# A diffusion layer's front: the order of context's sums of squares, of the query norms and of the chunk transpositions

## The chip, the cores and the metric

One NeuronCore of one Trainium2 chip. The time is the device time of one execution in microseconds (us), as the median of several runs. The engines are named as in the profile: PE (TensorE), DVE (VectorE), ACT (ScalarE), POOL (GpSimd), and SP, which issues most of the DMAs. PEld is the loading of weights into TensorE.

## The reference

One layer of a diffusion backbone on 512 latent tokens and 256 context tokens, D = 1024. What the change touches:

```python
h  = rms_norm(x, g_norm1) * (1.0 + sc1) + sh1          # latents
hc = rms_norm(ctx, g_norm1) * (1.0 + csc1) + csh1      # context; sc, sh from silu(c) @ w_ada
aq, ak, av, dq, dk, dv, dz, da, db, ga, gd = split_cols(h @ w_in)      # the same for hc
q_a = axial_rope(rms_norm(heads(aq, 8), q_norm_g), row, col)   # windowed attention
k_a = axial_rope(rms_norm(heads(ak, 2), k_norm_g), row, col)
o_dl = bidir_delta(...)     # gated DeltaNet, chunks of 64; each needs a triangular inverse
x_new = x + gt1 * merge(y_attn, o_dl, dz, ga, gd)
x_new = x_new + gt2 * mlp(x_new, sh2, sc2)
```

## The kernel before

Everything is held transposed, with features on the 128 partitions and tokens along the free axis. A product in full precision is made of three products of rounded halves: high by high, high by low and low by high (`split`, `wload`, `modulate`).

**How instructions get their order.** The program is traced in Python, and a planner then puts each engine's instructions in a fixed order at build time. Of the instructions that are ready in its own model of time, it takes the one that stands first in the program. So an instruction can stand ahead of others that come before it in the program, if the planner takes it to be ready earlier. What was planned runs in that order on its engine: one that is not ready on the chip holds up all behind it. `tc.add_manual_dep(..., nosync)` adds an edge that binds the planner only. `pm` uses it to chain TensorE's matmuls of the front in the very order of the program; a plain `PE.matmul` is not in that chain.

**The front** (lines 239 to 420). The modulation vectors come from `w_ada`, loaded in eight pieces of 1 MB (`wada(kt)`). For each of the eight feature tiles `kt`: `strip(kt)` multiplies the condition by its piece (16 TensorE instructions), `columns(kt)` turns the row into columns `modA` and `modS` by way of one ACT copy (L263), `latent(kt)` normalises and modulates the latents (L350 on DVE, L351 on ACT, L352 on DVE, L373 on ACT), and `big(kt, tiles...)` multiplies them into up to four accumulators of the DeltaNet's keys, three matmuls a tile. They are software pipelined: step `kt` of the loop issues columns(kt+1), strip(kt+2), latent(kt+1), big(kt, 0, 1, 2, 3). The matmuls of `strip`, `columns` and `big` go through `pm`.

`rms` makes the reciprocal root of a mean square: squares on ACT (L308), additions on DVE (L311), a matmul with ones that sums over the partitions (L313), then Ln and Exp on ACT (through `act`, L148). Context's is called in step 3 behind big(3, ...), with plain `PE.matmul`. `context(i)` modulates one of eight feature tiles of the context (L350, L351, L352, L364), two of them behind each of the steps 4 to 7. `ab_strips` multiplies latents, and behind big(7) context, by the small gate weights.

**Attention's inputs beside the chunk matrices** (lines 862 to 1041). `weave` runs two generators side by side in proportion to their numbers of steps. `mats` normalises the DeltaNet's keys and calls `chunk_mats(gi)` for three groups of chunks. Each makes products of keys in two banks `kk` (L850), decays by matmuls (L875, L876), and DVE products of both (L870, L874, L886, L888, L895, and last L896, which writes `NTO[gi]` and is the last reader of `kk`). `attn_in` goes through six tiles: the keys, three query tiles, the values, the last query tile. `in_tile_steps` yields behind every two of the eight feature tiles: a tile of latents alone has four matmuls to such a step in its first half, one with context eight. The previous tile's `finish` (k_attn, q_attn, v_attn) is called behind the first step of the next tile; q_attn and k_attn begin with `qk_norm`: square (ACT, L491), scaled copy (L492), a matmul that sums over a head (L494), rotation on DVE (L497 to L500), Ln, Exp, product (L505). The weights of a tile are cut by ACT (L280 high part, L286 the negated copy that a DMA then adds to).

Behind the weave, `fw` (L906) and `bw` (L909) transpose the first group's matrix on DVE, their sum (L1041) goes to `invert`, and two more pairs of transpositions follow before the second inversion.

Of the kernel before, what the change touches and what calls it, by code (L numbers as in the profile page):

```python
# [12 lines left out]
ALU = mybir.AluOpType  # L13
# [10 lines left out]
ATT = 32  # L24
NHALF = 3
CTXAT = 3
WARM = 3, 6, 4, 4
NONES = 16
AHEAD = 2
# [10 lines left out]
SEQ = 512  # L40
CTX = 256
# [4 lines left out]
HC = CH // 2  # L46
# [53 lines left out]
def tile_layer(ctx: ExitStack, tc: tile.TileContext, I: dict, out: bass.AP, dbg=None):  # L100
    nc = tc.nc
    V, A, G, PE = nc.vector, nc.scalar, nc.gpsimd, nc.tensor
# [19 lines left out]
    alloc, bank = mem.get, lambda n=1: banks.get(n * 512)  # L122
# [14 lines left out]
    nosync = mybir.DependencyInfo(mybir.DependencyClass.NoSync, mybir.DependencyReason.DATA)  # L137
    actg = {"set": None, "head": None, "ops": []}

    def act(out_, in_, func, **kw):  # L140

        sets = TABLES.get(func)
        if sets and actg["set"] not in sets:
            head = A.preload_act_table_set(sets[0])
            for o in actg["ops"]:
                tc.add_manual_dep(head.ins, o.name, nosync, reason="table sets")
            actg.update(set=sets[0], head=head.ins, ops=[head.ins])
        r = A.activation(out_, in_, func, **kw)  # L148
        if sets:
            tc.add_manual_dep(r.ins, actg["head"].name, nosync, reason="table sets")  # L150
            actg["ops"].append(r.ins)
        return r
# [4 lines left out]
    ones = const.tile([P, P], F32, name="ones")  # L157
# [61 lines left out]
    def strip(kt):  # L219

        if kt < 2:
            rps.append(banks.get(512, True))
        rp_ = rps[kt % 2]
        wb = wbs[kt % 4]
        for half in range(2):
            for g in range(4):
                k = half * 4 + g
                pm(rp_[32 * g:32 * g + 32, :256], scond[:, k], wb[:, k * 256:(k + 1) * 256],
                   start=(half == 0), stop=(half == 1))
        if kt < 4:  # L230
            wada(kt + 4)
        if kt > 3:
            wb.free()

    def warm(kt, n):

        for _ in range(n):
            pm(rps[kt % 2][:, 384:512], ones, ones, start=True, stop=True)

    xs_, cs_ = alloc(8 * SEQ), alloc(8 * CTX)  # L240
# [59 lines left out]
    rstd = alloc(768)  # L300
    rx, rc = rstd[:, :512], rstd[:, 512:768]

    def rms(src, nt, n, r):

        ss = bank()
        for i in range(nt):
            b = alloc(1024)
            A.activation(b.ap, src[:, i * 1024:(i + 1) * 1024], AF.Square)  # L308
            w = 512
            while w >= n:  # L310
                V.tensor_tensor(b[:, :w], b[:, :w], b[:, w:2 * w], op=ALU.add)  # L311
                w //= 2
            PE.matmul(ss[:, :n], ones, b[:, :n], start=(i == 0), stop=(i == nt - 1))  # L313
            b.free()
        act(r, ss[:, :n], AF.Ln, bias=epsc, scale=1.0 / D)
        ss.free()
        act(r, r, AF.Exp, scale=-0.5)

    rms(xs_, 4, SEQ, rx)
    strip(0)  # L320
    warm(0, WARM[0])
    columns(0)
# [26 lines left out]
    def modulate(t, src, r, sc, sh, hi, lo, eng=V):  # L349
        V.scalar_tensor_tensor(t, src, sc, r, op0=ALU.mult, op1=ALU.mult)  # L350
        A.activation(r32(hi), t, AF.Identity, bias=sh)  # L351
        eng.scalar_tensor_tensor(r32(lo), t, sh, hi, op0=ALU.add, op1=ALU.subtract)  # L352
        return r32(hi), r32(lo)
# [4 lines left out]
    def context(kt):  # L358

        t = alloc(256)  # L360
        o = kt * 512
        hc.append(modulate(t.ap, ct_[kt], rc, modA[:, kt, 1:2], modS[:, kt, 1:2],
                           HCb[:, o:o + 256], HCb[:, o + 256:o + 512]))
        tc_.append((t, A.activation(t.ap, t.ap, AF.Identity, bias=modS[:, kt, 1:2])))  # L364
# [11 lines left out]
    def big(kt, *tiles):  # L376

        for i in tiles:
            w, acc = early[i]
            for j, (x, y) in enumerate(((0, 0), (0, 1), (1, 0))):  # L380
                pm(acc.ap, w[x][:, kt, :], hx[kt][y], start=(kt == j == 0), stop=(kt == KT - 1 and j == 2))

    latent(0)
    load_early()
    warm(1, WARM[1])
    columns(1)
# [18 lines left out]
    for kt in range(3, KT):  # L405
        if kt + 1 < KT:
            columns(kt + 1)
        if kt + 2 < KT:
            strip(kt + 2)
        if kt + 1 < KT:  # L410
            latent(kt + 1)
        if kt == 5:
            abx = bank()
            ab_strips(abx.ap, tx, 0)
        big(kt, 0, 1, 2, 3)
        if kt == 3:
            rms(cs_, 2, CTX, rc)
        if kt > 3:
            for i in range(2):
                context(2 * kt - 8 + i)  # L420
    hold.append(tx[-1][1])
    ab_strips(abx.ap, tx, 1)
    abc = bank()
# [320 lines left out]
    t, t2 = alloc(TOK), alloc(TOK)  # L744
# [51 lines left out]
    for n in range(2):  # L796
        m = A.activation(trr[:, 2 * n:2 * n + 2], tri[:, 8 * n:8 * n + 2], AF.Copy)
# [6 lines left out]
    m = V.tensor_copy(maskb, mt.ap.rearrange("p (d k) -> p d k", d=2))  # L804
# [31 lines left out]
    NTO = [alloc(512, True) for _ in range(3)]  # L836
    v3 = lambda ap, n=HC: ap.rearrange("p (m i) -> p m i", i=n)
# [15 lines left out]
    def diag_off(dst):  # L853

        v = dst.ap.rearrange("p (m x i) -> p x m i", x=2, i=HC)
        return v[:, 0], v[:, 1]

    def chunk_mats(gi):
        ms = slice(gi * 16, gi * 16 + 16)
        kk = bank(2)  # L860
        kD, kO = diag_off(kk)
        for _ in half_products(kk, gi, kT):
            for _ in range(HPAUSE):
                yield
        yield
        dO = bank()
        for d in range(2):
            mg, mb = alloc(1024), alloc(512)
            row = lambda m_: m_[:, d, :].unsqueeze(1).broadcast_to([P, 16, HC])
            V.tensor_tensor(v3(mb.ap), row(nmask), bc(btok[:, d, ms], HC), op=ALU.mult)  # L870
            dp = bank()
            for x in range(2):
                gx = mg[:, x * 512:x * 512 + 512]
                V.tensor_tensor(v3(r32(gx)), row(mi), bc(gsp[:, x, d, ms], HC), op=ALU.mult)  # L874
                PE.matmul(dp.ap, trr[:, d, :], r32(gx), start=(x == 0), stop=(x == 1))  # L875
                PE.matmul(dO.ap, trr[:, 2 + d, :], r32(gx), start=(d == x == 0), stop=(d == x == 1))  # L876
            mg.free()
            if gi == 0:
                eb = alloc(512)
                e, na = eb.ap, neg[0][:, d * 512:d * 512 + 512]  # L880
            else:
                o = (gi - 1) * 512
                e, na = ED[d][:, o:o + 512], neg[1 + d][:, o:o + 512]
            act(e, dp.ap, AF.Exp)
            dp.free()
            V.tensor_tensor(e, e, mb.ap, op=ALU.mult)  # L886
            mb.free()
            V.tensor_tensor(v3(na), v3(e), kD, op=ALU.mult)  # L888
            if gi == 0:
                eb.free()  # L890
            yield
        eb = alloc(512) if gi == 0 else None
        e = eb.ap if gi == 0 else EO[:, (gi - 1) * 512:gi * 512]
        act(e, dO.ap, AF.Exp)
        V.tensor_tensor(v3(e), v3(e), bc(tbO[:, ms], HC), op=ALU.mult)  # L895
        V.tensor_tensor(v3(NTO[gi].ap), v3(e), kO, op=ALU.mult)  # L896
        for b in (kk, dO, eb):
            if b:
                b.free()
        yield  # L900


    mat = lambda ap: ap.rearrange("p (r s) -> p r s", s=HC)

    def fw(src, t):
        V.transpose(mat(t), src.rearrange("p (m i) -> p i m", i=HC))  # L906

    def bw(src, t):
        V.transpose(t.rearrange("p (j i) -> p i j", i=HC), src.rearrange("p (m i) -> p i m", i=HC))  # L909

    X, X3 = [], []

# [97 lines left out]
    def attn_in():  # L1010
        qs = [lambda acc, j=j: q_attn(acc, j) for j in range(4)]
        todo = [(T_AK, k_attn)] + [(T_AQ + j, qs[j]) for j in range(3)] + [(T_AV, v_attn), (T_AQ + 3, qs[3])]
        done = None
        for ti, finish in todo:
            g = in_tile_steps(ti, ti in (T_AK, T_AV))
            while True:
                try:
                    next(g)
                except StopIteration as e:
                    acc = e.value  # L1020
                    break
                if done:
                    done[0](done[1])
                done = None
                yield
            done = finish, acc
            if ti == T_AQ + 3:
                finish(acc)
            yield
# [316 lines left out]
    for g in range(2):  # L1346
        ms = slice(16 * g, 16 * g + 16)
        f, b = xa[0][:, ms], xa[1][:, ms]
# [57 lines left out]
    for g in range(2):  # L1406
        cs_ = slice(g * 1024, g * 1024 + 1024)
        V.tensor_tensor(nv(on[:, cs_]), nv(ot_[:, cs_]), bc(osf[:, g * 16:g * 16 + 16], HD), op=ALU.mult)

    for qq in range(2):  # L1410
# [3 lines left out]
        for a in range(2):  # L1414
            n = 2 * qq + a
            t = alloc(512)
# [50 lines left out]
    for ct in range(8 - NHALF):  # L1467
        w = wnext()
        acc = bank()
# [5 lines left out]
    rx = alloc(512)  # L1475
# [55 lines left out]
    for hf in range(4):  # L1531
        act_ = []
        for f in range(FT):
            if first:
                bufs, _, acc = first.pop(0)
            else:
                bufs = [alloc(1024), alloc(1024)]
                w = wload(I["wm1"][hf * FT + f], bufs=bufs)
                acc = bank()
                mm3(acc.ap, w, ms)  # L1540
            r, hl = alloc(1024), alloc(1024)
# [14 lines left out]
        for ct in range(8):  # L1556
            acc = bank()
# [119 lines left out]
```

## Time and profile before

| | us |
|---|---|
| three runs | 902.81, 903.33, 905.05 |
| median | 903.33 |
| the profiled execution | 903.9 |
| its span, first to last instruction | 902.1 |
| PE busy in the span | 875.8 |
| DVE busy | 579.3 |
| ACT busy | 456.7 |
| DMA engines | 119 GB/s mean |

The mean granted TensorE clock was 0.994 of full speed. A row of a timeline gives the start in us, the length, the engine and line, the operation, destination and sources, the size, and how many instructions are merged in it; in brackets stands how long the engine was idle before it and what it waited for. Where rows are merged, the length runs to the last one's end. A group of instructions gives busy us, mean ns of one, and the idle time before them. The engine of a row that ends in q (PEq, SPq) is that engine's queue or sequencer.

### The profile page before, as it was taken

What the parts mean: (1) busy time and instruction counts of PE and PEld (TensorE: products, weight loads), DVE (VectorE), ACT (ScalarE), POOL (GpSimd) and SP (SyncE); (2) the same over time, 40 slices, a digit from 0 to 9 for tenths busy, and PEclk for the clock granted to TensorE, in tenths of its full rate; (3) what the DMA queues carried; (4) which work ended last, traced back from release to release, by engine and by line L of the source; (5) the groups of instructions that cost most, each with busy time, mean ns of one, the idle gap of its engine ahead of it and who ended that gap; (6) DMA issues with size and microseconds to landing.
All of it is one profiled execution on the core that took longest, in us unless ns stands there. A gap on an engine that the chain in (4) does not pass through costs nothing.

```text
span 902.1 us, 16815 instructions
## 1 busy us (share of the span) xinstructions
PE 875.8 (97%) x7070; PEld 705.7 (78%) x7070; DVE 579.3 (64%) x991; ACT 456.7 (51%) x823; POOL 27.7 (3%) x43
## 2 busy tenths in 40 slices
PE   8899989999999999999999999999999999999998
PEld 5578768867777788777778899888888888888886
DVE  4477799886677997587777988831654235334511
ACT  6488756376669886466754345630452134113400
POOL 0010001010000001110000000000000000000000
PEclk9899999999999999999999999999999999999999
DMA  9851454533112133634216873730643234323011
GB/s 355 339 149 29 94 141 95 116 72 59 36 36 59 57 109 96 212 93 146 73 37 230 272 239 111 252 121 1 210 140 94 69 91 143 94 70 87 31 47 47
DMA packets 30892, 107.16 MB, mean 119 GB/s; under 512 B 3808, under 2 KB 4448, under 8 KB 29792
## 3 DMA queue, kind: packets, MB, share of 16 engines
q1 hardware_dynamic: 28368, 97.18, 32.9%
q0 software_dynamic: 2448, 8.91, 6.0%
q8 instruction: 55, 0.90, 0.4%
q14 instruction: 21, 0.17, 0.1%
HBM read 103.98 MB, written 2.10 MB: 118 GB/s over the span
## 4 chain that ended last, share of the span: by engine, by line
PE 84%; DVE 9%; ACT 4%; issue 2%; DMA 1%; SPq 0%; DVEq 0%; ACTq 0%
PE banks L345 15%; PE banks L346 15%; PE banks L347 15%; PE banks L1116 11%; PE banks L468 5%; PE banks L205 5%; PE banks L1161 3%; PE banks L473 2%; PE banks L624 2%; PE banks L1252 1%; PE banks L634 1%; PE banks L701 1%; PE banks L1273 1%; PE banks L1240 1%; ACT m L148 1%
## 5 line engine op out<-in xcount | busy, mean ns | idle before, releaser
L346 PE MATMUL banks<-m,m 128*128 128x512 f32 (+1 forms) x536 | 202.3, 380 | 0.0
L347 PE MATMUL banks<-m,m 128*128 128x512 f32 (+1 forms) x536 | 202.3, 380 | 0.0
L345 PE MATMUL banks<-m,m 128*128 128x512 f32 (+1 forms) x536 | 201.9, 380 | 0.3 <-ACT m L351 0.3
L280 ACT ACTIVATE m<-wr 128x1024 fp32r<-128x1024 f32 x68 | 71.6, 1057 | 156.2 <-PE banks L346 76.8
L289 DVE TENSOR_TENSOR m<-wr,m 128x1024 fp32r<-128x1024 f32 x68 | 82.8, 1224 | 68.0 <-PE banks L346 34.2
L345 PEld LDWEIGHTS banks<-m,m 128*128 128x128 f32 x536 | 100.0, 188 | 20.1 <-ACT m L351 0.7
L346 PEld LDWEIGHTS banks<-m,m 128*128 128x128 f32 x536 | 100.3, 188 | 19.4 <-DVE m L352 0.2
L347 PEld LDWEIGHTS banks<-m,m 128*128 128x128 f32 x536 | 100.3, 188 | 18.8
L1561 DVE SCALAR_TENSOR_TENSOR m<-banks,modT,m 128x512 f32<-128x512 f32 x32 | 24.0, 750 | 104.4 <-PE banks L347 104.4
L1116 PE MATMUL banks<-m,wh 128*128 128x512 f32 x320 | 85.0, 403 | 0.0
L468 PE MATMUL banks<-m,wh 128*128 128x512 f32 (+1 forms) x320 | 73.9, 372 | 1.4 <-DVE m L896 1.4
L280 ACT ACTIVATE wh<-wr 128x1024 fp32r<-128x1024 f32 (+1 forms) x58 | 54.6, 941 | 40.5 <-PE banks L346 11.2
L1116 PEld LDWEIGHTS banks<-m,wh 128*128 128x128 f32 x320 | 57.7, 188 | 12.7
L468 PEld LDWEIGHTS banks<-m,wh 128*128 128x128 f32 x320 | 52.8, 189 | 11.7 <-DVE m L896 1.8
L184 ACT ACTIVATE m<-m 128x512 fp32r<-128x512 f32 (+1 forms) x56 | 34.9, 629 | 43.0 <-DVE m L1544 21.4
L185 DVE TENSOR_TENSOR m<-m,m 128x512 fp32r<-128x512 f32 (+1 forms) x56 | 38.3, 689 | 20.1 <-ACT m L184 19.7
L205 PE MATMUL banks<-m,m 128*32 128x256 f32 (+3 forms) x352 | 49.3, 387 | 0.7 <-DMA m<-in_wada 0.4
L289 DVE TENSOR_TENSOR wl<-wr,wh 128x1024 fp32r<-128x1024 f32 (+1 forms) x41 | 41.6, 1014 | 11.6 <-PE banks L1116 8.7
L1182 DVE SCALAR_TENSOR_TENSOR m<-wa,m 128x1024 f32<-128x1024 f32 x32 | 39.0, 1222 | 15.3 <-DMA wa<-in_wada 15.2
L205 PEld LDWEIGHTS banks<-m,m 128*128 128x128 f32 (+1 forms) x352 | 34.2, 158 | 13.9 <-issue 5.3
L1116 PE MATMUL banks<-m,wl 128*128 128x512 f32 x160 | 43.5, 399 | 0.0
L345 PE MATMUL banks<-m,wh 128*128 128x512 f32 (+1 forms) x120 | 41.7, 349 | 0.0
(242 smaller groups left out, 1439.1 us busy)
## 6 DMA issues: line engine op xcount, KB each, us to landing
wr<-in_wm SPq DMA_DIRECT2D x64, 512.0 KB, 3.6
wr<-in_win SPq DMA_DIRECT2D x38, 512.0 KB, 3.7
wa<-in_wada SPq DMA_DIRECT2D x32, 512.0 KB, 4.2
wl<-in_win POOLq DMA_DIRECT2D x17, 512.0 KB, 5.4
m<-in_wada SPq DMA_DIRECT2D x8, 1024.0 KB, 13.9
m<-in_xT SPq DMA_DIRECT2D x8, 512.0 KB, 6.0
wr<-in_wbr SPq DMA_DIRECT2D x16, 256.0 KB, 2.7
wr<-in_wout SPq DMA_DIRECT2D x8, 512.0 KB, 4.7
```

Of the source, the lines that this page charges most:

```text
L184: A.activation(r32(hi), src, AF.Copy)
L185: return (eng or V).tensor_tensor(r32(lo), src, hi, op=ALU.subtract)
L205: m = PE.matmul(*args, **kw)
L280: h = A.activation(r32(hi), raw, AF.Copy)
L289: V.tensor_tensor(r32(lo), raw, hi, op=ALU.subtract)
L345: mm(acc, w[0][:, k, :], xhi, start=(start and i == 0), stop=False)
L346: mm(acc, w[0][:, k, :], xlo, start=False, stop=False)
L347: mm(acc, w[1][:, k, :], xhi, start=False, stop=(stop and i == n - 1))
L468: PE.matmul(a, w[0][:, k, :], x, start=(k == 0 and x is xs[k][0]), stop=False)
L1116: PE.matmul(acc.ap, w[x][:, k, :], hx[k][y], start=(p == 0), stop=(p == 3 * KT - 1))
L1161: PE.matmul(pa.ap, w[x][:, j, :], r32(Q[y][:, :, j, :]), start=(j == p == 0), stop=(j == 3 and p == 2))
L1182: V.scalar_tensor_tensor(t.ap, wa, 0.5, scr.ap, op0=ALU.mult, op1=ALU.mult, accum_out=modT[:, grp, j:j + 1])
```

## The change

Three parts.

1. Context's sums of squares. The old `rms` is cut in two: `squares` yields the added squares, `rms` sums them over the partitions with a matmul function that the caller gives. Latents still use `PE.matmul`. For context, the squares are traced in step 4 (not 3) ahead of big, and the two sums go through `pm`, between big(4, 0, 1) and big(4, 2, 3): TensorE's explicit order holds them there. The eight context tiles are spread as 1, 3, 2, 2 over the steps 4 to 7, where it was 2, 2, 2, 2.
2. `attn_in` calls the previous tile's finish behind the second step of the next tile instead of the first: behind eight matmuls of a tile of latents, or sixteen of one with context. The last query tile's is still called at once.
3. `chunk_mats` remembers its last DVE product (L896), and every `fw` and `bw` gets an edge behind it that binds the planner.

No arithmetic is added or removed.

```diff
+CTXS = {3: (), 4: (0,), 5: (1, 2, 3), 6: (4, 5), 7: (6, 7)}
...
-    def rms(src, nt, n, r):
-
-        ss = bank()
+    def squares(src, nt, n):
+
         for i in range(nt):
             b = alloc(1024)
             A.activation(b.ap, src[:, i * 1024:(i + 1) * 1024], AF.Square)
...
-            PE.matmul(ss[:, :n], ones, b[:, :n], start=(i == 0), stop=(i == nt - 1))
+            yield b
+
+    def rms(sq, nt, n, r, mm):
+
+        ss = bank()
+        for i, b in enumerate(sq):
+            mm(ss[:, :n], ones, b[:, :n], start=(i == 0), stop=(i == nt - 1))
             b.free()
...
-    rms(xs_, 4, SEQ, rx)
+    rms(squares(xs_, 4, SEQ), 4, SEQ, rx, PE.matmul)
...
-        big(kt, 0, 1, 2, 3)
-        if kt == 3:
-            rms(cs_, 2, CTX, rc)
-        if kt > 3:
-            for i in range(2):
-                context(2 * kt - 8 + i)
+        if kt == 4:
+            csq = list(squares(cs_, 2, CTX))
+        big(kt, 0, 1)
+        if kt == 4:
+            rms(csq, 2, CTX, rc, pm)
+        big(kt, 2, 3)
+        for i in CTXS[kt]:
+            context(i)
...
+    last_ = []
...
-        V.tensor_tensor(v3(NTO[gi].ap), v3(e), kO, op=ALU.mult)
+        m = V.tensor_tensor(v3(NTO[gi].ap), v3(e), kO, op=ALU.mult)
+        last_[:] = [m]
...
     def fw(src, t):
-        V.transpose(mat(t), src.rearrange("p (m i) -> p i m", i=HC))
+        m = V.transpose(mat(t), src.rearrange("p (m i) -> p i m", i=HC))
+        tc.add_manual_dep(m.ins, last_[0].ins.name, nosync, reason="behind the chunks")
...
-        done = None
+        done, left = None, 0
...
-                if done:
+                left -= 1
+                if done and not left:
                     done[0](done[1])
-                done = None
                 yield
-            done = finish, acc
+            done, left = (finish, acc), 2
```

`bw` gets the same edge as `fw`.

More of the change, by code (lines that the diff above doesn't have):

```diff
@@ L905, in fw @@
     def fw(src, t):
-        V.transpose(mat(t), src.rearrange("p (m i) -> p i m", i=HC))
+        m = V.transpose(mat(t), src.rearrange("p (m i) -> p i m", i=HC))
+        tc.add_manual_dep(m.ins, last_[0].ins.name, nosync, reason="behind the chunks")
     def bw(src, t):
-        V.transpose(t.rearrange("p (j i) -> p i j", i=HC), src.rearrange("p (m i) -> p i m", i=HC))
+        m = V.transpose(t.rearrange("p (j i) -> p i j", i=HC), src.rearrange("p (m i) -> p i m", i=HC))
+        tc.add_manual_dep(m.ins, last_[0].ins.name, nosync, reason="behind the chunks")
     X, X3 = [], []
```

## The prediction

> **What bounds it now.** I read the page first, then the busy time by stage, the waits of TensorE, and only then the timelines of the stages that the diff touches.
>
> ```profile
> span 902.1 us, 16815 instructions
> ...
> PE 875.8 (97%) x7070; PEld 705.7 (78%) x7070; DVE 579.3 (64%) x991; ACT 456.7 (51%) x823; POOL 27.7 (3%) x43
> ```
>
> TensorE (PE) is busy for 97% of the span, so time can only come from its 26 us of idleness, or from matmuls that run slowly. By stage (columns: stretch, its length, busy us and count of PE, weight loads, DVE, ACT, POOL, then granted clock, DMA share, GB/s):
>
> ```profile
> 33.60:45.00 11.40, 7.87 (x41) 5.09 (x40) 3.61 (x8) 3.04 (x6) 0.00 (x0) 0.70 0.68 267
> ...
> 103.00:135.00 32.00, 28.51 (x356) 21.04 (x354) 31.78 (x50) 19.59 (x29) 2.59 (x3) 1.00 0.55 132
> 135.00:182.00 47.00, 47.00 (x267) 39.61 (x266) 43.09 (x101) 24.25 (x38) 4.32 (x5) 1.00 0.50 102
> ```
>
> Two stages with idle PE are touched. In 33.6 to 45 all engines idle and the clock is down. In 103 to 135 VectorE (DVE) is full and PE waits 3.5 us; straight behind it PE is full for 47 us, so there it has work in hand that a saved wait brings forward. Of PE's waits two groups are used below (sum, times, longest), beside those that the timelines show:
>
> ```profile
> PE banks L634 <- ACT m L148: 2.6, 2, 2.1
> PE banks L494 <- ACT m L491: 2.1, 3, 1.2
> ```
>
> **Context's squares (the large term).** PE in the front:
>
> ```profile
> 37.18 1.19 PE L313 MATMUL banks<-m,ones 128*128 128x256 f32 x2 [3.53 <-DVE m L311]
> 38.30 5.97 PE L205 MATMUL banks<-m,m 128*32 128x256 f32 x28
> 44.11 0.59 PE L313 MATMUL banks<-m,ones 128*128 128x256 f32 x2
> 44.54 0.50 PE L205 MATMUL banks<-c_prm,m 128*128 128x2 f32 x4
> 44.98 4.02 PE L205 MATMUL banks<-m,m 128*32 128x256 f32 x28
> 48.83 0.50 PE L205 MATMUL banks<-c_prm,m 128*128 128x2 f32 x4
> ```
>
> The first product of the sum (L313, from rms of context) was planned ahead of strip 5 and the products of big(3), and PE stands from 33.65 to 37.18 for VectorE's additions. Strip 5 needs none of that. The clock falls behind it:
>
> ```profile
> 33.65:37.18 3.53, 0.01 (x1) 0.03 (x1) 3.41 (x8) 2.35 (x4) 0.00 (x0) 0.79 1.01 417
> ...
> 38.30:40.20 1.90, 1.90 (x18) 0.63 (x17) 0.00 (x0) 0.00 (x0) 0.00 (x0) 0.50 1.08 410
> ```
>
> 28 instructions (a strip's 16 and 12 of big) take 5.97 us from 38.30 and 4.02 us from 44.98; by starts, 44.98 to 48.83, they take 3.85. With 0.43 for an L313 pair (44.11 to the next start, 44.54) and 0.44 for columns, the way from 37.18 to 44.98 would be 0.43+3.85+0.43+0.44 = 5.15 warm; it took 7.80. So the stall cost 3.53 + 2.65 = 6.18 us.
>
> With the sums in the explicit order behind big(4, 0, 1), what is late next? Strips wait for their weights (issue, then us to landing, of w_ada's pieces 5 and 6):
>
> ```profile
> 19.58 0.33 SPq L217 DMA_DIRECT2D m<-in_wada  x1
> ...
> 20.90 0.33 SPq L217 DMA_DIRECT2D m<-in_wada  x1
> ```
> ```profile
> m<-in_wada SPq DMA_DIRECT2D x1, 1024.0 KB, 14.3
> m<-in_wada SPq DMA_DIRECT2D x1, 1024.0 KB, 15.5
> ```
>
> Piece 5 lands at 33.9: PE waits 0.25 us instead of 3.53. Piece 6 lands at 36.4; strip 6 comes at 33.9+3.85+0.44 = 38.2, so it waits for nothing. Then the strip and half of big (1.07+1.39) put L313 at 40.7. Its operands:
>
> ```profile
> 32.67 1.99 ACT L308 ACTIVATE m<-m 128x1024 f32<-128x1024 f32 x2
> ...
> 36.62 0.76 DVE L311 TENSOR_TENSOR m<-m 128x256 f32<-128x256 f32 x2
> ...
> 45.25 0.42 ACT L148 ACTIVATE m<-m 128x256 f32<-128x256 f32 x1
> ...
> 58.31 0.49 ACT L364 ACTIVATE m<-m,modS 128x256 f32<-128x256 f32 x1
> ```
>
> The squares ran at 32.67 though program order has them behind latent(4): they fill an idle ACT once context is there, and I take them to stay, ready at 37.4. Were they planned behind latent(5) (its tail near 40), 2.0 of ACT and 0.76 of DVE would put them at 42.8, 1 to 2 us late. Columns(6) then comes at 42.9 against 48.83: 5.93 us earlier, which is 6.18 less 0.25.
>
> The other side: context's modulation starts when rc is there, 45.67 before, now about 42.55 (L313 done at 41.5, then Ln and Exp). Relative to PE that is 2.8 us later. VectorE's load between (groups from 45 to 59, then the whole stretch, and PE's first weights for context's strips behind big(7)):
>
> ```profile
> L350 DVE SCALAR_TENSOR_TENSOR m<-m,modA,m 128x256 f32<-128x256 f32 x8 | 3.6, 477 | 0.0
> L352 DVE SCALAR_TENSOR_TENSOR m<-m,modS,m 128x256 fp32r<-128x256 f32 x8 | 3.5, 476 | 0.3 <-ACT m L351 0.3
> L352 DVE SCALAR_TENSOR_TENSOR m<-m,modS,m 128x512 fp32r<-128x512 f32 x3 | 2.2, 748 | 0.4 <-ACT m L351 0.4
> L350 DVE SCALAR_TENSOR_TENSOR m<-m,modA,m 128x512 f32<-128x512 f32 x3 | 2.2, 739 | 0.0
> ```
> ```profile
> 45.25:58.80 13.55, 13.55 (x91) 10.03 (x84) 11.96 (x30) 12.30 (x27) 0.00 (x0) 1.00 0.39 137
> ```
> ```profile
> 60.51 0.13 PEld L205 LDWEIGHTS banks<-m,m 128*32 128x32 f32 x4 [0.30 <-issue]
> ```
>
> In it stand eight contexts (7.1 us) and three latents (about 1.5 each). After the change latent 5 is done by then, so 1.7 us falls away (1.5 at the filling of 11.96 in 13.55): 11.85 us, from 42.55 to 54.4, where the last context's row (L364) ended at 58.80 before. Its products came at 60.51 and would come at 54.6. That is 0.2 us of slack against 1.7 before; with latent 7 perhaps queued behind a context I charge 0.5 us (between 0 and 3). Moving one context from step 4 to step 5 changes only where it stands in this queue.
>
> Net of the front: 5.9 - 0.5 = 5.4 us. What follows is fed by these same engines, so it moves along.
>
> **The transpositions.** PE, then DVE, then ACT:
>
> ```profile
> 126.26 3.85 PE L468 MATMUL banks<-m,wh 128*128 128x512 f32 x16
> 131.50 2.13 PE L468 MATMUL banks<-m,wh 128*128 128x512 f32 x10 [1.40 <-DVE m L896]
> ```
> ```profile
> 126.37 2.12 DVE L906 STREAM_TRANSPOSE m<-m 128x1024 f32<-128x1024 f32 x1
> ...
> 130.77 0.68 DVE L896 TENSOR_TENSOR m<-m,banks 128x512 f32<-128x512 f32 x1
> 131.37 2.17 DVE L909 STREAM_TRANSPOSE m<-m 128x1024 f32<-128x1024 f32 x1
> ```
> ```profile
> 130.19 1.06 ACT L280 ACTIVATE wh<-wr 128x1024 fp32r<-128x1024 f32 x1 [2.15 <-issue]
> ...
> 133.57 0.60 ACT L491 ACTIVATE m<-banks 128x512 f32<-128x512 f32 x1 [2.32 <-DVE m L909]
> ```
>
> L906 stands inside the last chunk's work; L896, the chunk's last reader of its banks, ends at 131.45, and PE waits 1.40 us for it. Behind L896, L906 gives back 2.04 us to it (129.4, before PE's sixteen products end at 130.1), and L906 and L909 follow back to back and end where they did. So the inversion loses nothing and PE gains up to 1.40. Against that: some of the next ten products belong to the following tile, whose high weights are ready only at 131.25 (L280); if they come first, PE still waits 1.15 and gains 0.25. I take 1.2 (range 0.25 to 1.4), since sixteen products of the half-filled tile need only L896.
>
> **The norms.** A key or query norm's product (L494) is now issued behind eight products of the next tile, not four:
>
> ```profile
> 93.34 1.19 PE L468 MATMUL banks<-m,wh 128*128 128x512 f32 x4
> 94.38 1.45 PE L494 MATMUL banks<-m,c_bones 128*128 128x512 f32 x4
> ...
> 103.31 1.98 PE L468 MATMUL banks<-m,wh 128*128 128x512 f32 x8
> 106.44 1.12 PE L494 MATMUL banks<-m,c_bones 128*128 128x512 f32 x2 [1.16 <-ACT m L491]
> ```
>
> The first query norm already stands behind eight, and still waits 1.16 for its square (L491): the later place in the program need not move it. If every L494 went four products back (0.92 us by the eight from 103.31), the waits of 2.1 would shrink by at most 1.85. The key norm, behind four now, moves back 0.92 and takes a DVE that is full from 103 on with it; that loses at most 0.9. I take 0.
>
> **Sum.** 5.4 + 1.2 + 0 = 6.6 us. The profiled execution took 903.9 us (span 902.1 and 1.8 around it), 0.6 above the median of 903.33; against the median I forecast 896.7.
>
> **The clock rule.** The rows show 1.00 until the stall, 0.50 behind it, and 2.65 us of slow matmuls. The Trainium skill (TensorE: Matmul & The Clock Gate, Part 1) says the clock halves after an idle window of about 3.4 us that runs freely, whatever the kernel does. By that rule a gap of 3.53 would rarely hold a whole window, and most timed executions would not pay the 2.65. The trace agrees on the half rate; that the drop is rare no run here shows, and the three times, 902.81 to 905.05, differ by 2.24.
>
> **Rivals.**
> The clock holds in the timed runs: if the 2.65 belongs to some executions only, 6.6 - 2.65 = 3.95 remain: 899.4. For it: the spread of the times. Against: the one trace shows the drop.
> Contexts late: the 0.5 becomes 3, as ACT and DVE are near full in 45 to 59: 899.2.
> Norms gain too: 1.85 more, 894.9.
> Given back: the attention's units in 182 to 260 are fed a unit ahead, and PE's transpositions (L634) wait once for exponentials (L148), 2.1 us, in a plan drawn anew. Two to four such waits take back 4.2 to 8.4: 903.
> Slower: the units lose their lead. If the later norms push the scores back in the plan, so that each of the eight units waits those 2.1 us, 16.8 - 6.6 = 10.2 us are lost: 913.5. It decides from the fifth unit on (10.5 us, 3.9 more than the gain). Against both: the scores wait for the last query tile, whose norm is issued where it was.
>
> **Numbers.** Forecast 0.60 (895 to 898.7); clock 0.10; contexts 0.12; norms 0.08; given back 0.06; slower 0.04. From norms to contexts, with the ends of the small terms, is 894 to 901. A difference of 0.3%, 2.7 us, is about what a measurement of this kernel can tell from none. Faster than that 0.88, within it 0.08, slower 0.04.
>
> **What will show it.** L313 without a wait and behind six products of big(4); a clock of 1.00 from 33 to 45; columns(6) near 43; no wait for context's rows near 54.6, or one under 1 us; L906 and L909 back to back behind L896, without PE's wait for it; L494 behind eight products with waits near those of before. A wait of big(7) or context's strips over 2 us, or squares planned behind latent 5, would make the forecast wrong upward.

## The result, and the profile after

The changed kernel took 898.59 us in the median of six runs (897.99 to 901.04), the kernel before 903.80 beside it (902.81 to 905.69). The ratio is 0.9943, with a 95% interval of 0.9927 to 0.9959: 5.2 us faster, where 6.6 were forecast. The profiled execution was the slowest of the six, 901.04 us, so its span tells less than the median does.

After the change lines stand 1 to 13 further down: context's L313 and the other matmuls of the front are now L206 (the helper `pm`), L350 and L352 are L356 and L358, L468 is L476, L491 and L494 are L499 and L502, L505 is L513, L896 is L906, `fw` and `bw` are L917 and L921, the inversion's L929 is L942. From the page of after:

```profile
span 899.3 us, 16815 instructions
...
PE 876.0 (97%) x7070; PEld 705.3 (78%) x7070; DVE 579.0 (64%) x991; ACT 456.4 (51%) x823; POOL 27.6 (3%) x43
```

PE's busy time is that of before within 0.2 us; idle time went. The two stages by windows of after (columns as in the prediction), the second moved by the 4 to 5 us that PE leads there, and 1 us longer:

```profile
33.60:45.00 11.40, 11.30 (x91) 8.04 (x95) 7.95 (x20) 6.88 (x14) 0.28 (x1) 1.00 0.82 323
98.00:131.00 33.00, 29.82 (x362) 21.93 (x361) 32.01 (x49) 21.37 (x33) 2.59 (x3) 1.00 0.54 128
```

In the front PE goes from 7.87 busy us and 41 instructions to 11.30 and 91, and the clock from 0.70 to 1.00. In the second stage PE still idles 3.2 us (3.5 before). PE's timeline of after in the front:

```profile
34.03 4.06 PE L206 MATMUL banks<-m,m 128*32 128x256 f32 x28
...
38.35 2.68 PE L206 MATMUL banks<-m,m 128*32 128x256 f32 x22
40.87 1.02 PE L206 MATMUL banks<-m,ones 128*128 128x256 f32 x4
41.54 1.74 PE L206 MATMUL banks<-m,m 128*128 128x512 f32 x6
43.12 0.50 PE L206 MATMUL banks<-c_prm,m 128*128 128x2 f32 x4
...
52.42 7.71 PE L206 MATMUL banks<-m,m 128*128 128x512 f32 x59 [0.29 <-DVE m L358]
60.07 1.48 PE L206 MATMUL banks<-m,four 128*32 128x512 f32 x4
```

The two sums (`ones`) stand at 40.87 behind 22 instructions, a strip's 16 and six products of big(4), and wait for nothing. The same row `four` of before:

```profile
64.97 1.48 PE L205 MATMUL banks<-m,four 128*32 128x512 f32 x4
```

PE's lead is 48.83 - 43.12 = 5.71 us at columns(6) and 64.97 - 60.07 = 4.90 here. The 0.8 between went behind the contexts, which DVE now does ahead of latent 7 (after):

```profile
47.79 1.66 DVE L358 SCALAR_TENSOR_TENSOR m<-m,modS,m 128x256 fp32r<-128x256 f32 x4
...
51.62 0.75 DVE L358 SCALAR_TENSOR_TENSOR m<-m,modS,m 128x512 fp32r<-128x512 f32 x1
```

Context's squares stayed early, and the first weights of context's strips wait for no data (after, ACT and PE's weight loads):

```profile
32.95 1.99 ACT L308 ACTIVATE m<-m 128x1024 f32<-128x1024 f32 x2
```
```profile
55.60 0.13 PEld L206 LDWEIGHTS banks<-m,m 128*32 128x32 f32 x4 [0.30 <-issue]
```

The stage of the transpositions and norms in after, PE, DVE and ACT:

```profile
91.63 1.45 PE L502 MATMUL banks<-m,c_bones 128*128 128x512 f32 x4
102.24 1.13 PE L502 MATMUL banks<-m,c_bones 128*128 128x512 f32 x2 [0.99 <-ACT m L499]
...
122.01 7.09 PE L476 MATMUL banks<-m,wh 128*128 128x512 f32 x33
130.44 1.13 PE L502 MATMUL banks<-m,c_bones 128*128 128x512 f32 x2 [1.33 <-ACT m L499]
```
```profile
94.30 1.03 DVE L513 TENSOR_TENSOR m<-m 128x512 f32<-128x512 f32 x2 [1.61 <-ACT m L149]
...
125.06 0.69 DVE L906 TENSOR_TENSOR m<-m,banks 128x512 f32<-128x512 f32 x1
125.66 2.08 DVE L917 STREAM_TRANSPOSE m<-m 128x1024 f32<-128x1024 f32 x1
127.67 2.09 DVE L921 STREAM_TRANSPOSE m<-m 128x1024 f32<-128x1024 f32 x1
...
131.63 0.19 DVE L942 TENSOR_TENSOR m<-m 128x30 f32<-128x30 f32 x1
```
```profile
129.79 0.60 ACT L499 ACTIVATE m<-banks 128x512 f32<-128x512 f32 x1 [2.82 <-DVE m L921]
```

L917 and L921 stand back to back behind L906, and 33 products run from 122.01 without the wait that was there. But 8 us later PE waits 1.33 for a query norm's square (L499), and that square waited 2.82 for the second transposition (L921).

In the profiled executions PE's lead is 4.9 us at the transposes of the values (143.7 to 138.8), 5.0 at the first attention unit (181.0 to 176.0), 4.3 at 257, and 2.8 at the end (spans 902.1 and 899.3). Of the last loss most is this execution's clock, which fell at 394 (after):

```profile
392.00:396.00 4.00, 3.04 (x55) 2.26 (x59) 1.97 (x6) 2.74 (x10) 0.16 (x1) 0.78 0.00 0
396.00:400.00 4.00, 4.00 (x125) 3.35 (x119) 3.18 (x9) 2.82 (x9) 0.00 (x0) 0.80 0.02 4
```

The mean clock differs from run to run, and the runs can be sorted by it:

| kernel | runs | lowest to highest clock | median | span at 0.998 |
|---|---|---|---|---|
| before | 67 | 0.990 to 0.998 | 0.994 | 900.0 to 901.4 |
| changed | 17 | 0.994 to 1.000 | 0.998 | 897.0 to 898.2 |

At an equal clock the change is worth about 3 us; the rest of the 5.2 is the clock. Not one of the 67 runs of before, which stood beside the experiments below, came above 0.998.

### The profile page after: what moved, and what is told of

The parts are those of the page before. It is cut to its first block, busy times and chain, and to the rows that moved or that the text cites. A ratio compares the mean times of both kernels' runs of the same rounds, so it can differ in the third digit from the quotient of the medians.

```text
span 899.3 us, 16815 instructions
## 1 busy us (share of the span) xinstructions
PE 876.0 (97%) x7070; PEld 705.3 (78%) x7070; DVE 579.0 (64%) x991; ACT 456.4 (51%) x823; POOL 27.6 (3%) x43
## 4 chain that ended last, share of the span: by engine, by line
PE 77%; DVE 14%; ACT 5%; issue 2%; DMA 2%; SPq 0%; DVEq 0%; ACTq 0%
PE banks L353 15%; PE banks L352 15%; PE banks L351 15%; PE banks L1129 11%; PE banks L206 4%; PE banks L1174 3%; PE banks L476 2%; PE banks L632 2%; PE banks L1265 1%; PE banks L642 1%; DVE m L186 1%; ACT m L149 1%; PE banks L1286 1%; DVE m L943 1%; DVE m L942 1%
## 5 line engine op out<-in xcount | busy, mean ns | idle before, releaser
L352 PE MATMUL banks<-m,m 128*128 128x512 f32 (+1 forms) x536 | 202.3, 380 | 0.0
L352 PEld LDWEIGHTS banks<-m,m 128*128 128x128 f32 x536 | 100.3, 188 | 19.3 <-DVE m L358 0.2
L476 PE MATMUL banks<-m,wh 128*128 128x512 f32 (+1 forms) x320 | 74.3, 373 | 0.0
L476 PEld LDWEIGHTS banks<-m,wh 128*128 128x128 f32 x320 | 53.1, 189 | 10.3 <-issue 1.7
L206 PE MATMUL banks<-m,m 128*32 128x256 f32 (+3 forms) x352 | 48.3, 373 | 1.1 <-DVE m L358 0.5
L206 PEld LDWEIGHTS banks<-m,m 128*128 128x128 f32 (+1 forms) x352 | 33.1, 153 | 13.4 <-issue 4.0
L353 PE MATMUL banks<-m,wl 128*128 128x512 f32 (+1 forms) x120 | 41.7, 349 | 0.6 <-DVE wl L290 0.6
```

The lines of the kernel that those rows point to most:

```text
L206: m = PE.matmul(*args, **kw)
L352: mm(acc, w[0][:, k, :], xlo, start=False, stop=False)
L353: mm(acc, w[1][:, k, :], xhi, start=False, stop=(stop and i == n - 1))
L476: PE.matmul(a, w[0][:, k, :], x, start=(k == 0 and x is xs[k][0]), stop=False)
```

## The experiments

Three questions: which part carries the gain, where the transpositions' 1.2 us went, and whether the timed runs too pay the slow matmuls behind the wait, or only some executions do.

### Which part: each alone, and two together

The front alone (`e1_front`), from the changed kernel:

```diff
-            done, left = (finish, acc), 2
+            done, left = (finish, acc), 1
...
-        tc.add_manual_dep(m.ins, last_[0].ins.name, nosync, reason="behind the chunks")
```

> Context's sums alone in TensorE's explicit order; norms and transpositions as before. Theory A (the front carries the whole gain; the other two parts cancel): 4.9 to 5.4 us faster, about 898.6, the same as the whole change. Theory B (all three parts gain, and something later takes part back): 3.5 us faster or less, about 900.3. Columns(6) near 43.1 in both.

Measured: 899.37 beside 904.28, ratio 0.9944 (0.9922 to 0.9966). The front alone gives what the whole change gives, as far as the intervals tell. PE in this kernel:

```profile
42.57 0.50 PE L206 MATMUL banks<-c_prm,m 128*128 128x2 f32 x4
...
126.03 2.13 PE L476 MATMUL banks<-m,wh 128*128 128x512 f32 x10 [1.40 <-DVE m L906]
```

Columns(6) is early, and the chunk's wait of 1.40 is still there, to the hundredth.

The transpositions alone (`e2_transp`): the kernel before with the two edges of `fw` and `bw`.

> The transpositions alone behind the last chunk. Theory A: PE's wait of 1.40 us for the chunk's last product goes and the first norm waits are as before, so 1.0 to 1.4 us faster (about 902.6). Theory B: the query norm behind it (L494 of before), which waits for the second transposition, takes the 1.40 us as its own wait: 0.0 to 0.3 us faster.

Measured: 904.46 beside 904.28, ratio 0.9996 (0.9980 to 1.0011). No gain shows, though the interval would still hold the 1.2 us that were forecast; so the rows decide. PE, DVE and ACT in this kernel:

```profile
129.34 2.93 PE L474 MATMUL banks<-m,wh 128*128 128x512 f32 x15 [0.51 <-DVE m L904]
133.96 1.12 PE L500 MATMUL banks<-m,c_bones 128*128 128x512 f32 x2 [1.68 <-ACT m L497]
```
```profile
131.18 2.09 DVE L919 STREAM_TRANSPOSE m<-m 128x1024 f32<-128x1024 f32 x1
```
```profile
133.31 0.60 ACT L497 ACTIVATE m<-banks 128x512 f32<-128x512 f32 x1 [5.63 <-DVE m L919]
```

The norm's row in the kernel before is

```profile
134.22 1.12 PE L494 MATMUL banks<-m,c_bones 128*128 128x512 f32 x2 [0.58 <-ACT m L491]
```

The wait for the chunk fell from 1.40 to 0.51, and the query norm's rose from 0.58 to 1.68: the sum, 1.98, is 2.19 now. The norm's square is written into memory that the transposition still reads. It waits 5.63 us for L919 to end at 133.27 and starts at 133.31. (That it waits for the memory, and not for data, is tested below.)

The norms alone (`e3_norms`): the kernel before with `left` and the 2.

> The norms alone behind the second step of the next tile. Theory A: the key norm's sum comes about 1 us later and VectorE, which is full behind it, starts the inversion about 1.1 us later; TensorE waits for it: 0.5 to 1.1 us slower (about 904.6). Theory B: no change within 0.3 us, since the query norms already stood behind eight products.

Measured: 906.87 beside 904.28, ratio 1.0042 (1.0024 to 1.0061): 2.6 us slower, for a reason that neither theory had. PE and a window in this kernel:

```profile
134.11 0.80 PE L479 MATMUL banks<-m,wl 128*128 128x512 f32 x1 [3.44 <-DMA wl<-in_win]
```
```profile
136.00:140.00 4.00, 4.00 (x14) 3.42 (x14) 2.83 (x9) 0.00 (x0) 0.00 (x0) 0.50 0.01 4
```

The planner, with the finishes moved, put a product of the value tile's low weights ahead of the norm, and on the chip the DMA that completes those weights is late. PE waits 3.44 us and then runs at half the clock. This execution, at 910.49, is 3.6 us above the median of its kernel; that the other runs wait like this is not shown, but their mean clock fits it (median 0.992, before 0.994). In the profiled execution of the whole change no such wait is among PE's.

Front and transpositions together (`e4_front_transp`): the changed kernel with `left` at 1.

> Front and transpositions, without the norms. Theory A: 6 to 6.6 us faster (about 897.5), 1 us better than the whole change. Theory B: 4.9 to 5.3 us faster, the same as the whole change.

Measured: 898.63 beside 904.28, ratio 0.9936 (0.9918 to 0.9953), not to be told from the whole change or from the front alone. PE and DVE in this kernel:

```profile
124.71 2.94 PE L476 MATMUL banks<-m,wh 128*128 128x512 f32 x15 [0.52 <-DVE m L906]
129.32 1.12 PE L502 MATMUL banks<-m,c_bones 128*128 128x512 f32 x2 [1.67 <-ACT m L499]
```
```profile
130.51 0.20 DVE L942 TENSOR_TENSOR m<-m 128x30 f32<-128x30 f32 x1
```

The same exchange of waits as alone. And the inversion starts (L942) at 130.51, against 131.63 with the norms moved as well: what the norms cost DVE is 1.1 us in these two executions. The row of before is 135.41:

```profile
135.41 0.18 DVE L929 TENSOR_TENSOR m<-m 128x30 f32<-128x30 f32 x1
```

### Where the transpositions' gain went

If the square waits because its memory is still being read, giving that memory back later should free it. `e7_late_free` is `e4_front_transp` with

```diff
-    xb.free()
-    neg[0].free()
...
     weave((att, 48 - ATT), (inv, INV[1]))
+    xb.free()
+    neg[0].free()
```

> Front and transpositions without the norms, and the first group's two matrices are freed only behind the attention's inputs, so that the third query norm does not get their memory. Theory A (that norm waits for the second transposition only through the reused memory, and this is where the transpositions' gain went): the 1.67 us of TensorE's wait for it shrink below 0.5, and the time is 1 to 1.5 us under front and transpositions alone. Theory B: VectorE, full until then, is late for another reader instead, and the wait only moves: no gain beyond 0.5 us.

Measured: 905.54 beside 904.29, ratio 1.0006 (0.9991 to 1.0021). The waits of PE in this kernel, then the same groups in `e4_front_transp` (sum, times, longest):

```profile
PE banks L502 <- ACT m L499: 1.8, 3, 1.2
PE banks L1265 <- DVE m L1258: 7.0, 4, 4.5
```
```profile
PE banks L502 <- ACT m L499: 3.2, 3, 1.7
PE banks L1265 <- DVE m L1258: 2.8, 3, 1.8
```

In time nothing is gained over before. Locally it did what was asked: the norms' waits fell from 3.2 to 1.8 us, and the square of the third query norm no longer waits. ACT in `e7_late_free`:

```profile
122.63 0.60 ACT L499 ACTIVATE m<-banks 128x512 f32<-128x512 f32 x1
```

The square runs 5.8 us ahead of the end of the second transposition (L921, from 126.26 to 128.47 there). So it needs none of its data, and the memory is what held it. PE gains less than the norms' waits lost, for it now waits 1.14 us for ACT's copy of the values (L544): the last query tile's norm comes 0.92 us earlier than in `e4_front_transp` (139.38 and 140.30), and 0.32 of that was there at the key norm already (89.07 and 89.39), so 0.6 us are gained. With the memory held longer the planner drew the rest anew: PE's waits for L1258, a step of the DeltaNet's recurrence, grow by 4.2 us, the longest, of 4.55, at 394.5. By stretches of 25 us (PE, granted clock, DMA share, GB/s), `e7_late_free`:

```profile
225.00:250.00 25.00, 22.92 (x135) 0.93 0.18 32
...
375.00:400.00 25.00, 20.35 (x347) 0.93 0.27 88
...
425.00:450.00 25.00, 23.06 (x464) 0.93 0.26 81
```

In three stretches the clock is 0.93, which is 0.07 x 25 = 1.75 us each; in the profiled execution of `e4_front_transp`, the shortest of its six, it is 1.00 in all of them. The fall near 235 is in nine of the eleven traces, so it is not of this plan. By 470 the local gain is a loss of 7 us in these two executions (the same products at 469.95 and 462.49), and of all runs of this kernel none came above a clock of 0.996. So 0.6 us were had at the transpositions by this way, which the time does not show; what the whole 1.4 us of the norms' waits would be worth stays open.

### Is the slow clock in the timed runs?

`e5_stall` was to be the yardstick: the kernel before with context's two sums bound by `pm` at the places that the planner had chosen. `e6_filled` adds twelve products that nothing uses (`warm(5, 12)`; in `e5_stall` it is `warm(5, 0)`), so that PE is not idle during the wait.

```diff
+        if kt == 3:
+            csq = list(squares(cs_, 2, CTX))
+            css = bank()
+            warm(5, 12)
+            pm(css[:, :CTX], ones, csq[0][:, :CTX], start=True, stop=False)
...
         big(kt, 0, 1, 2, 3)
         if kt == 3:
-            rms(cs_, 2, CTX, rc)
+            pm(css[:, :CTX], ones, csq[1][:, :CTX], start=False, stop=True)
```

> The kernel before, with its two sums of context's squares bound by the explicit order to the very places that the planner had given them (the first ahead of strip 5, the second behind big(3)); norms and transpositions as before. Both theories: the time of before within 0.5 us, TensorE idle for 3.5 us from about 33.7, the granted clock 0.50 behind it. It is the yardstick for the next run.

> The same, with twelve unused products of ones by ones (about 0.27 us each, 3.2 us in all) issued ahead of the first sum: the sum still waits for VectorE until 37.4, but TensorE does not idle. Theory A (half of the front's cost is the clock, which falls because of the idle stretch): the clock stays at 1.00 there, 2.65 us are saved where the sums stand still, and the time comes 2.5 to 3.5 us under that of the stalled kernel. Theory B (the clock falls by itself in windows of a fixed length and would fall elsewhere): the same time as the stalled kernel within 0.7 us.

Measured: 901.85 and 900.77 beside 904.29; ratios 0.9976 (0.9961 to 0.9991) and 0.9957 (0.9943 to 0.9971). The yardstick missed: with other places in the program DVE's additions were planned earlier, and the wait is 2.26 us, not 3.5. The time is 2.4 us under before, where no difference was expected. PE and a window of `e5_stall`:

```profile
36.12 1.19 PE L206 MATMUL banks<-m,ones 128*128 128x256 f32 x2 [2.26 <-DVE m L311]
```
```profile
36.00:40.00 4.00, 3.88 (x20) 1.90 (x21) 1.58 (x3) 1.39 (x3) 0.00 (x0) 0.50 1.03 392
```

The clock fell all the same. In the profiled executions columns(6) is 2.5 us earlier with the filling (48.20 and 45.72), the medians differ by 1.1 and their intervals overlap: undecided.

`e10_filled` repeats it with the planned order of before kept on every engine, except for the 13 unused products in the wait: strip(5) is traced behind the first sum, where the planner had it.

```diff
-        if kt + 2 < KT:
+        if kt + 2 < KT and kt != 3:
...
+            warm(5, 13)
+            pm(css[:, :CTX], ones, csq[0][:, :CTX], start=True, stop=False)
+            strip(5)
```

> The kernel before, instruction for instruction in its planned order on every engine, with thirteen unused products of ones by ones put into TensorE's 3.5 us of waiting ahead of the first of context's two sums. Theory A (the clock is a good half of the front's cost): the granted clock stays at 1.00 from 33 to 45, the way from the first sum to columns(6) shortens by 2.65 us, and the time comes 2 to 3 us under before (ratio 0.997 to 0.998), though the sum waits for VectorE as long as ever. Theory B (windows of low clock only move elsewhere, or only some executions lose the clock there): within 0.8 us of before.

Measured: 900.66 beside 903.13, ratio 0.9966 (0.9954 to 0.9978). PE and a window of this kernel:

```profile
34.67 3.15 PE L206 MATMUL banks<-ones 128*128 128x128 f32 x26
38.34 0.67 PE L206 MATMUL banks<-m,ones 128*128 128x256 f32 x2 [0.52 <-DVE m L311]
38.94 4.01 PE L206 MATMUL banks<-m,m 128*32 128x256 f32 x28
...
43.66 4.02 PE L206 MATMUL banks<-m,m 128*32 128x256 f32 x28
```
```profile
38.30:40.20 1.90, 1.86 (x19) 0.98 (x20) 0.23 (x1) 0.12 (x1) 0.00 (x0) 1.00 1.10 400
```

The wait for DVE's additions is as long as before; it is only filled, for all but 0.52. (The sum stands 1.16 us later than in before's profile because this execution was 1.18 us late already: columns(3) at 30.70 and 29.52.) Strip 5 with its products takes 4.01 us, not 5.97, and from the first sum to strip 6 it is 5.32 us (38.34 to 43.66), not 7.80. These 2.48 us are the clock's share in one pair of traces; the medians differ by 2.47. So the clock's share is in the timed runs.

### The whole change again

`e8_whole` is the changed kernel unaltered, beside `e5_stall` to `e7_late_free`.

> The whole change once more, as the yardstick on this chip: 5.0 us faster than before (0.994), and in executions with a granted clock of 1.00 a span of 896.2 us. Theory A (the clock decides the spread): in every kernel of this call the span grows by about one us for each us of missing clock. Theory B: the spread does not follow the clock.

Measured: 899.89 beside 904.29, ratio 0.9947 (0.9929 to 0.9965), as at first. Its two executions at a clock of 1.000 have a span of 895.8 us. Over all 17 runs of the changed kernel the mean span is 896.0 at a clock of 1.000, 897.6 at 0.998 and 899.1 at 0.996, which is 0.9 us for each us of missing clock; in before it is 900.6 at 0.998 and 903.2 at 0.994, which is 0.7. So the spread follows the clock in the main. A wait that the prediction named stands in PE's timeline of this run, with the clock behind it:

```profile
235.52 2.05 PE L642 MATMUL banks<-c_ident,m 128*128 128x128 f32 x10 [2.08 <-ACT m L149]
```
```profile
236.00:240.00 4.00, 4.00 (x20) 3.49 (x19) 3.05 (x5) 2.85 (x5) 0.00 (x0) 0.58 0.86 131
```

It is there before and after alike (two waits, 2.6 us in sum), so it explains no difference, but it is the next place where idle time can cost nearly twice. The clock fell behind it in nine of the eleven traces. Filling it was not tried.

## Why the prediction came out as it did

**Right: the front.** The sums came at 40.87 (40.7 forecast) and columns(6) at 43.12 (42.9); the lead there is 5.71 us of 5.93, and the execution of after stood 0.28 us later already ahead of the change (columns(4) at 33.43 and 33.15). The squares stayed where an idle ACT takes them. Alone, this part gives the whole gain.

**Right: its two halves.** The forecast split the front into idle time, 3.28 less 0.5 for late contexts, and 2.65 of slow matmuls. At an equal clock the changed kernel is 3 us shorter, and `e10_filled`, which mends only the clock, gains 2.5. The 2.65 itself is one execution's: with the same wait of 3.53 us the way from the first sum to strip 6 took 6.88 us in `e2_transp` (37.75 to 44.63) and 6.74 in `e3_norms` (38.18 to 44.92), which is 1.7 and 1.6 over the 5.15 of a full clock. The rival in which the clock holds in the timed runs falls with `e10_filled`, and with 67 runs of before of which none came above 0.998. Its chance of 0.10 rested on the spread of the times. That comes in good part from other places: the clock fell between 234 and 247 in nine of the eleven traces, and between 365 and 404 in seven.

**Nearly right: late contexts.** 0.8 us was lost, for 0.5 charged. It was not at context's own rows, which nothing waits for, but by the path that the charge named: latent 7 queued behind contexts on DVE.

**Wrong: the transpositions, 1.2 us taken and none found.** PE's lead is 4.9 us ahead of this stage and behind it. The edge did what was forecast: the two transpositions back to back, and the chunk's wait gone. The step that failed is "the inversion loses nothing and PE gains up to 1.40". It asked who else waits for L906 and L909 only as far as the inversion. The row quoted there, L491 with 2.32 us idle for L909, says that the next query norm's square waits for the second transposition too. That one still ends last, so PE's wait moves from the chunk to the norm: 1.40 and 0.58 became 0.51 and 1.68. The range down to 0.25 did not hold 0.

**Not measurable: the norms, 0 taken.** The products are issued behind eight others and still wait, 1.33 and 0.99 us for the two largest. The bounded loss was real: the key norm's product is 2.75 us earlier (94.38 to 91.63) where PE leads by 4.9, so 2.1 late; DVE then waits 1.61 for its root and 0.50 for the first query norm's copy, and the inversion starts 1.1 us later than without this part. In the time, 0.9943 against 0.9936, it doesn't show. Alone this part costs 2.6 us, by its one trace through a late DMA that the forecast had in no case; that the whole change escapes it is a matter of the plan.

**Sum.** Forecast 5.4 + 1.2 + 0 = 6.6; measured 4.9 + 0 + 0 = 4.9 by the front alone and 5.2 by the whole. The contexts' rival at 899.2 lies nearer to the measured 898.59 than the forecast of 896.7 does, but by another mechanism: its 3 us did not come, and the missing 1.4 is about 1.2 of the transpositions and 0.3 of the contexts. 898.59 lies within 895 to 898.7 by 0.1 us only; with one of three terms wrong, that is in part luck.

**The clock rule.** The Trainium skill (TensorE: Matmul & The Clock Gate, Part 1) speaks of a free-running window of about 3.4 us. The traces agree. In each of the eleven, the stretches at half rate start on a grid of 3.41 us that runs through the whole execution, and inside the kernel they last one or two steps of it. One step at half rate loses 1.7 us, 0.002 of 900 us, and the mean clocks lie mostly at 0.994, 0.996, 0.998 and 1.000. But the window that makes the clock fall need not be idle throughout. By the profile's busy time, all 22 falls ahead of the kernels' ends stand behind a step of the grid in which PE was busy for 7 to 52%, and of the more than 2800 steps at full rate without a fall behind them none was busy for less than 48%. So it matters how a wait lies on the grid. In `e8_whole` the wait of 2.08 us lies within one step (232.52 to 235.93, PE busy for 1.33 us), and the clock falls. In `e4_front_transp` the same wait, of 2.07, is divided between two steps, and the clock stays at 1.00:

```profile
231.19:234.60 3.41, 2.21 (x15) 1.42 (x12) 3.23 (x6) 2.09 (x4) 0.00 (x0) 1.00 0.01 2
234.60:238.01 3.41, 2.45 (x17) 1.94 (x18) 2.96 (x8) 2.98 (x8) 0.86 (x1) 1.00 0.47 50
```

The conclusion that the prediction weighed, that most executions would escape the drop, doesn't hold here: a wait of 3.53 us leaves PE idle for half of one step or more, wherever it lies. Nor is 3.4 us of idleness the least that is needed: waits of 2.26 and 2.08 us had the clock at 0.50 and 0.58 behind them.

## What to carry to other kernels

A wait of TensorE can cost far more than its length: where it left TensorE idle for half or more of a 3.41 us step, the matmuls of the next step ran at half rate, which loses up to 1.7 us, and twice in a row up to 3.4. A wait of 2 us was enough when it lay badly, and behind each of the five of 3.4 us or more the clock fell. Look at the granted clock just behind each wait, and if the wait can't be removed, products that nothing uses can fill it. Before moving an instruction behind another on a full engine, list everything that waits for the moved one's end, reuse of its memory included: a wait goes away only if its last cause does. In a kernel whose order a planner draws, an edge with a local gain can cost more somewhere else, so look for new waits over the whole span.

## What the hardware showed that was not expected

- The clock fell to 0.50 behind a wait of 2.26 us (`e5_stall`) and to 0.58 behind one of 2.08 (`e8_whole`), but not behind the same wait in `e4_front_transp`; the prediction had thought of 3.5 us. In eleven traces all falls stood behind a step of a fixed 3.41 us grid in which PE was busy for at most 52%.
- The spread of a one-core kernel's times is mostly the clock. Over 67 runs of before the mean clock is 0.990 to 0.998 and the span 899.8 to 907.3; at 0.998 alone it is 900.0 to 901.4.
- 13 unused products in a wait made the kernel 2.5 us faster (ratio 0.9966, 0.9954 to 0.9978) with the wait itself left as long as it was.
- PE waited 3.44 us for the DMA that completes low weights when one of their products was planned ahead of a norm (`e3_norms`).
